# Two of the four weight-block sums of a seven-product FFN chunk pair, formed by adding transfers instead of VectorE

## The chip, the cores and the metric

The kernel runs on one core of one Trainium2 chip. The metric is the device time of one execution in microseconds (us), from repeated runs; for a one-core program that is the time of that core. Before the change the median of three runs is 2695.78 us (2693.13 to 2700.33).

## The reference

Two blocks run one after the other on a (512, 1024) activation: a first block of dilated attention and a gated linear recurrence, and two layers of FFN, token mix, FFN. The change touches only the FFN:

```
def _swiglu(h, w_gate, w_up, w_down):
    return (jax.nn.silu(h @ w_gate) * (h @ w_up)) @ w_down
...
    h = _rmsnorm(x, norm_g[l, 0]) * (1.0 + sc0) + sh0
    x = x + 0.5 * g0 * _swiglu(h, ffn_w_gate[l, 0], ffn_w_up[l, 0], ffn_w_down[l, 0])
```

There are four such FFNs (two layers, two each), with w_gate and w_up of 1024 x 2816 and w_down of 2816 x 1024, all fp32.

## The kernel before, in words

Activations lie transposed in SBUF, features on the 128 partitions and the 512 positions along the free axis. Every fp32 weight is split into a rounded part "hi" (written by ScalarE, L399) and a remainder "lo" (VectorE subtracts, L400), and a product is the sum of three passes hi*x_hi, lo*x_hi, hi*x_lo on TensorE.

Three of the four FFNs run in `ffn7` (L1343). Its 22 column blocks of 128 go two at a time; such a pair of blocks is called a chunk here. The first two chunks (blocks 0 to 3) are plain. Each of the nine others is computed by `seven` (L1391): the eight block products of [gate; up] with the two halves of the features and the two halves of the positions are replaced by seven products of 24 matmuls of 256 columns each (`prod`, L1378, matmul at L1385). With A11, A12 the two halves of the gate weights (512 features each), and p21, p22 those of the up weights, the weight-side sums are made in SBUF, on VectorE: s1 = p21 + p22 (two instructions, L1410), S3 = p21 + A11 in place (L1411), S2 = A11 + s1 in place (two, L1413), S4 = A12 + S2 in place (L1417).

Each of the seven products is a step with three stages: a load, a split (with sums ahead of it where there are any), and a run on TensorE. `ahead = 3` (L1550) puts the load stage 6 steps and the split stage 3 steps before the run stage. Between the second and the third step of the first chunk of each group of four blocks stand four `down` steps (L1483), the w_down products of the group before (matmul at L1504). So one group of two chunks is, on TensorE: A11, A12, four downs, S2, S1, S3, S4, A22, then A11', A12', S2', S1', S3', S4', A22' (a prime marks the second chunk). The groups of an `ffn7` are blocks 4-8, 8-12, 12-16, the single chunk 16-18, and 18-22: nine chunks, of which four are second in their group; in three `ffn7`, 27 chunks and 12 second ones.

Buffers: `raw` (the gate weights of a chunk, 1 MB) has 2; pieces `pc` of 512 KB (the up halves and the down weights, `piece`, L1336) rotate over 3 (`mraw` two, `macc` one); `hi` and `lo` have 4 each; `s` tiles (128x512) 40. All loads are issued by SP, in one queue, in order; a load waits there until its buffer is free, and everything behind it waits too. The order on each engine is set by the framework that places instructions, from the program's order and its own estimate of when each can start; it isn't always the order in which the code calls them. POOL has no work in the stretches of `seven`.

Of the kernel before, what the change touches and what calls it, by code (L numbers as in the profile page):

```python
# [11 lines left out]
ALU = mybir.AluOpType  # L12
# [282 lines left out]
class Prog:  # L295
# [1047 lines left out]
    def ffn7(self, l, s, h, nxt):  # L1343


        nc, A = self.nc, self.A
        wg, wu, wd = (A[f"ffn_w_{n}_2"][l, s // 2] for n in ("gate", "up", "down"))
# [30 lines left out]
        def prod(ps, w, x, first, last=True):  # L1378
            hi, lo = w
            for f in range(2):  # L1380
                cs = slice(f * 128, f * 128 + 128)
                o = ps[:, f * 256:(f + 1) * 256]
                for i, (a, b) in enumerate(((hi, x[0]), (lo, x[0]), (hi, x[1]))):
                    for k in range(4):
                        mm(o, a[:, k, cs], b[k], start=(first and f == i == k == 0), stop=(last and i == 2 and k == 3),  # L1385
                           skip_group_check=True)

        def parts():
            return [self.wp.tile([128, 4, 256], F32R, name=self.nm(n), tag=n) for n in ("hi", "lo")]

        def seven(f, dst):  # L1391

            cs = slice(f * 128, f * 128 + 256)
            u = {}

            def load_g():
                u["g"] = self.wload([(0, wg[:, cs])], KD, 256)

            def load_u():
                u["u"] = [self.piece(wu[a:a + 512, cs], 4) for a in (0, 512)]  # L1400

            def a1(i):
                return u["g"][:, 4 * i:4 * i + 4, :]

            def sums():

                p21, p22 = u["u"]
                u["s1"] = [self.s(shape=(128, 2, 256)) for _ in range(2)]
                for i in range(2):
                    nc.vector.tensor_add(u["s1"][i], p21[:, 2 * i:2 * i + 2, :], p22[:, 2 * i:2 * i + 2, :])  # L1410
                nc.vector.tensor_add(p21, p21, a1(0))  # L1411
                for i in range(2):
                    nc.vector.tensor_add(a1(0)[:, 2 * i:2 * i + 2, :], a1(0)[:, 2 * i:2 * i + 2, :], u["s1"][i])  # L1413

            def sum4():

                nc.vector.tensor_add(a1(1), a1(1), a1(0))  # L1417

            def whole(key, src, before=None):
                def g():  # L1420
                    if before:
                        before()
                    u[key] = parts()
                    self.split(src(), *u[key])
                return g

            def split1():
                u["S1"] = hi, lo = parts()
                for i in range(2):
                    self.split(u["s1"][i], hi[:, 2 * i:2 * i + 2, :], lo[:, 2 * i:2 * i + 2, :])  # L1430

            def copy(key, bank):
                u[key] = self.s()
                nc.scalar.activation(u[key], u[bank], AF.Copy)

            def run1():
                u["a"] = self.acc()
                prod(u["a"], u["A11"], forms.b11, True)
                copy("p1", "a")

            def run2():
                u["b"] = self.att()
                prod(u["b"], u["A12"], forms.b21, True)
                nc.vector.tensor_add(u["p1"], u["p1"], u["b"])

            def run6():
                prod(u["a"], u["S2"], forms.t2, False)
                copy("p2", "a")

            def run5():  # L1450
                u["c"] = self.att()
                prod(u["c"], u["S1"], forms.t1, True)
                copy("p5", "c")

            def run7():
                prod(u["a"], u["S3"], forms.t3, False)
                copy("p3", "a")
                nc.vector.tensor_add(u["p3"], u["p3"], u["p5"])

            def run3():  # L1460
                prod(u["c"], u["S4"], forms.b22, False)
                nc.vector.tensor_add(u["p2"], u["p2"], u["c"])

            def run4():
                prod(u["a"], u["A22"], forms.t4, False)

                aa = dst()
                for hf, (g, up) in ((1, (u["p2"], u["p3"])), (0, (u["p1"], u["a"]))):
                    t = self.s()
                    nc.scalar.activation(t, g, AF.Tanh, scale=0.5)  # L1470
                    nc.vector.scalar_tensor_tensor(t, t, 1.0, g, op0=ALU.add, op1=ALU.mult)
                    nc.vector.tensor_mul(t, t, up)
                    hi, lo = (d[:, hf].rearrange("p f n -> p (f n)") for d in aa)
                    nc.scalar.activation(hi, t, AF.Copy, scale=-1.0)
                    nc.vector.scalar_tensor_tensor(lo, t, -1.0, hi.bitcast(F32), op0=ALU.mult, op1=ALU.subtract)

            no = lambda: None
            return [(load_g, whole("A11", lambda: a1(0)), run1), (no, whole("A12", lambda: a1(1)), run2),
                    (load_u, whole("S2", lambda: a1(0), sums), run6), (no, split1, run5),
                    (no, whole("S3", lambda: u["u"][0]), run7), (no, whole("S4", lambda: a1(1), sum4), run3),  # L1480
                    (no, whole("A22", lambda: u["u"][1]), run4)]
# [35 lines left out]
        cs = slice(256, 512)  # L1517
# [3 lines left out]
        for m in range(2):  # L1521
            ms = slice(m * 128, m * 128 + 128)
            ps = []
            for r in range(2):
# [6 lines left out]
                p = self.acc() if r == 0 else self.att()  # L1531
# [4 lines left out]
        i = 3 * l + s + 1  # L1536
        steps, before = [], down(0, 4, aa)
        for f0, f1 in ((4, 8), (8, 12), (12, 16), (16, 18), (18, 22)):
            aa = []

            def dst(aa=aa):
                aa.append(a_tiles())
                return aa[-1]
# [624 lines left out]
```

## Time and profile before

| | |
|---|---|
| median of 3 runs | 2695.78 us |
| the profiled execution's own time | 2695.07 us |
| its span, first to last instruction | 2693.3 us |
| PE (TensorE) busy | 2605.3 us, 97% |
| DVE (VectorE) busy | 1973.2 us, 73% |
| ACT (ScalarE) busy | 1165.9 us, 43% |
| POOL busy | 322.5 us, 12% |
| moved by DMA | 339.70 MB, mean 126 GB/s |

The span is what the profile covers; 1.8 us of the execution's time lie around it. Busy shares are averages over stages that differ, so what a change is worth is read in its own stage.

### The profile page before, as it was taken

Reading aid. Unit: us, or ns where it says so; the run is one execution under the profiler, and the core shown is the slowest. Engines: PE = TensorE matmul, PEld = TensorE weight load, DVE = VectorE, ACT = ScalarE, POOL = GpSimd, SP = SyncE. Lnnn points to the kernel's source line nnn. Section 1 sums busy time; section 2 is a strip of 40 time slices with the busy share of each in tenths; the row PEclk is TensorE's granted clock in tenths of the full one; section 3 lists DMA queues with packets and bytes.
Section 4 is the critical chain, followed back from the end, with each engine's and each line's share of the span. In section 5 each row is a group of like instructions: output and inputs, shape, how many; then the busy total and the mean of one; then the engine's idle time right before and its main releaser. Section 6 shows DMA issues by size and latency. Waiting matters only on the chain.

```text
span 2693.3 us, 40840 instructions
## 1 busy us (share of the span) xinstructions
PE 2605.3 (97%) x15952; PEld 2275.8 (85%) x15952; DVE 1973.2 (73%) x3401; ACT 1165.9 (43%) x2112; POOL 322.5 (12%) x425
## 2 busy tenths in 40 slices
PE   7999989999999999999999999999999999999998
PEld 5878767789877889987889999999999887889998
DVE  8776784745878645689677778777777689677776
ACT  5322242634322224456544445444444557444434
POOL 4010010102100002232300000100002423200001
PEclk9999999999999999999999999999999999999999
DMA  9766645233467423631223324133233622123321
GB/s 274 255 203 204 229 138 187 79 114 106 152 223 242 155 88 103 178 90 50 87 66 101 116 86 148 53 106 95 90 112 89 177 63 64 56 94 102 111 94 63
DMA packets 317233, 339.70 MB, mean 126 GB/s; under 512 B 22128, under 2 KB 287856, under 8 KB 317040
## 3 DMA queue, kind: packets, MB, share of 16 engines
q1 hardware_dynamic: 317040, 337.10, 39.8%
q8 instruction: 125, 2.05, 0.3%
q14 instruction: 68, 0.56, 0.1%
HBM read 328.67 MB, written 8.39 MB: 125 GB/s over the span
## 4 chain that ended last, share of the span: by engine, by line
PE 70%; DVE 13%; DMA 10%; issue 4%; ACT 2%; POOL 1%; SPq 0%; DVEq 0%; POOLq 0%; ACTq 0%
PE att L1504 10%; PE acc L1385 9%; DMA mraw<-in_w_ada 8%; PE att L1385 7%; PE acc L417 6%; PE acc L415 6%; PE acc L419 6%; DVE lo L400 3%; DVE macc L656 2%; PE acc L467 2%; PE acc L573 2%; PE acc L575 2%; PE acc L577 2%; PE att L1955 2%; PE att L1939 1%
## 5 line engine op out<-in xcount | busy, mean ns | idle before, releaser
L399 ACT ACTIVATE hi<-raw 128x1024 fp32r<-128x1024 f32 (+2 forms) x329 | 327.0, 995 | 472.7 <-PE acc L419 137.6
L400 DVE TENSOR_TENSOR lo<-raw,hi 128x1024 fp32r<-128x1024 f32 (+2 forms) x329 | 378.9, 1154 | 114.9 <-ACT hi L399 108.6
L415 PE MATMUL acc<-s,hi 128*128 128x512 f32 x1008 | 272.6, 405 | 15.8 <-ACT s L399 7.4
L417 PE MATMUL acc<-s,lo 128*128 128x512 f32 x1008 | 266.4, 400 | 0.0
L419 PE MATMUL acc<-s,hi 128*128 128x512 f32 x1008 | 260.0, 394 | 0.0
L130 POOL TENSOR_TENSOR q<-q,q 128x256 f32<-128x256 f32 x96 | 80.6, 840 | 1482.4 <-ACT q L125 1481.3
L1385 PE MATMUL acc<-s,hi 128*128 128x256 f32 x1728 | 253.1, 281 | 0.0
L656 DVE SCALAR_TENSOR_TENSOR macc<-mraw,cs,macc 128x1024 f32<-128x1024 f32 x133 | 171.2, 1287 | 102.4 <-DMA mraw<-in_w_ada 98.7
L415 PEld LDWEIGHTS acc<-s,hi 128*128 128x128 f32 x1008 | 188.8, 191 | 61.5 <-ACT s L399 8.6
L417 PEld LDWEIGHTS acc<-s,lo 128*128 128x128 f32 x1008 | 192.0, 191 | 45.7 <-issue 0.5
L1385 PEld LDWEIGHTS acc<-s,hi 128*128 128x128 f32 x1728 | 226.4, 189 | 1.5
L419 PEld LDWEIGHTS acc<-s,hi 128*128 128x128 f32 x1008 | 189.9, 189 | 43.6
L400 DVE TENSOR_TENSOR lo<-pc,hi 128x1024 fp32r<-128x1024 f32 (+1 forms) x138 | 156.1, 1132 | 51.7 <-ACT hi L399 51.2
L1385 PE MATMUL att<-s,hi 128*128 128x256 f32 x1296 | 192.5, 281 | 0.0
L399 ACT ACTIVATE hi<-pc 128x1024 fp32r<-128x1024 f32 (+1 forms) x138 | 135.1, 981 | 109.7 <-PE att L1504 53.0
L1385 PEld LDWEIGHTS att<-s,hi 128*128 128x128 f32 x1296 | 169.9, 189 | 0.0
L1504 PE MATMUL att<-sm,hi 128*128 128x512 f32 x528 | 146.4, 393 | 0.0
L1259 DVE SCALAR_TENSOR_TENSOR x<-att,der,x 128x512 f32<-128x512 f32 x120 | 88.5, 748 | 67.6 <-PE att L1504 67.5
L1385 PE MATMUL acc<-s,lo 128*128 128x256 f32 x864 | 137.1, 280 | 0.0
L1259 DVE SCALAR_TENSOR_TENSOR x<-acc,der,x 128x256 f32<-128x256 f32 (+1 forms) x136 | 75.8, 560 | 77.3 <-PE acc L577 52.1
L1385 PEld LDWEIGHTS acc<-s,lo 128*128 128x128 f32 x864 | 117.3, 188 | 0.0
L1504 PEld LDWEIGHTS att<-sm,hi 128*128 128x128 f32 x528 | 98.5, 188 | 22.2
(491 smaller groups left out, 5485.1 us busy)
## 6 DMA issues: line engine op xcount, KB each, us to landing
mraw<-in_w_ada SPq DMA_DIRECT2D x144, 512.0 KB, 4.3
raw<-in_ffn_w_gate SPq DMA_DIRECT2D x44, 1024.0 KB, 5.2
raw<-in_w_in SPq DMA_DIRECT2D x30, 1024.0 KB, 5.5
pc<-in_ffn_w_up SPq DMA_DIRECT2D x60, 512.0 KB, 3.6
pc<-in_ffn_w_down SPq DMA_DIRECT2D x60, 512.0 KB, 3.6
raw<-in_w_in SPq DMA_DIRECT2D x46, 512.0 KB, 5.2
raw<-in_ffn_w_up SPq DMA_DIRECT2D x14, 1024.0 KB, 6.9
raw<-in_ffn_w_down SPq DMA_DIRECT2D x12, 768.0 KB, 5.2
```

What stands on the lines that cost most here:

```text
L130: nc.gpsimd.tensor_tensor(parts[-1], parts[-1], sq, op=ALU.add)
L399: self.nc.scalar.activation(hi, src, AF.Copy)
L400: self.nc.vector.tensor_sub(lo, src, hi.bitcast(F32))
L415: mm(ps, hi[:, k, :], xh[k], start=(k == 0), stop=False)
L417: mm(ps, lo[:, k, :], xh[k], start=False, stop=False)
L419: self.last_mm = mm(ps, hi[:, k, :], xl[k], start=False, stop=(k == kc - 1)).ins
L467: self.last_mm = mm(ps, x[k][:, ts], ws[k // 4][part][:, k % 4, :], start=(i == 0 and k == 0), stop=(i == 2 and k == KD - 1)).ins
L573: mm(ps, hi[k], ah[k], start=(k == 0), stop=False)
L656: nc.vector.scalar_tensor_tensor(st["acc"], raw, cs[:, k:k + 1], st["acc"], op0=ALU.mult, op1=ALU.add)
L1259: self.nc.vector.scalar_tensor_tensor(x, ps, gate[:, c:c + 1], x, op0=ALU.mult, op1=ALU.add)
L1385: mm(o, a[:, k, cs], b[k], start=(first and f == i == k == 0), stop=(last and i == 2 and k == 3), skip_group_check=True)
L1504: mm(ps.rearrange("p (a n) -> p a n", a=2), w[:, k, cs], aa[k // 2][x][:, :, k % 2, :], start=(i == k == 0), stop=(i == 2 and k == kc - 1))
```

## The change

`load_u` now brings the up weights so that two of the sums are formed by the transfers. The tile that becomes S3 is filled with p21 by SP as before, and then a transfer issued by POOL adds the A11 half of the gate weights to it, from DRAM. The two halves of s1 become `s` tiles that SP fills with p21 (a second reading of it, two loads of 256 KB), to which two POOL transfers add p22. p22 itself is still loaded by SP. The VectorE instructions of L1410 and L1411 are gone; those of L1413 and L1417 stay (in the new file they stand 8 lines further down, at L1421 and L1425, as all that follows them does).

```
             def load_u():
-                u["u"] = [self.piece(wu[a:a + 512, cs], 4) for a in (0, 512)]
+
+                up = [wu[a:a + 512, cs] for a in (0, 512)]
+                s3 = self.piece(up[0], 4)
+                u["s1"] = [self.s(shape=(128, 2, 256)) for _ in range(2)]
+                for add, ap, s3_ap in ((False, up[0], None), (True, up[1], wg[0:512, cs])):
+                    for i in range(2):
+                        src = ap[i * 256:i * 256 + 256].rearrange("(k p) n -> p k n", p=128)
+                        if add:
+                            nc.gpsimd.dma_start(u["s1"][i], src, accum_op=ALU.add)
+                        else:
+                            nc.sync.dma_start(u["s1"][i], src)
+                    if add:
+                        nc.gpsimd.dma_start(s3, s3_ap.rearrange("(k p) n -> p k n", p=128), accum_op=ALU.add)
+                u["u"] = [s3, self.piece(up[1], 4)]
...
             def sums():

-                p21, p22 = u["u"]
-                u["s1"] = [self.s(shape=(128, 2, 256)) for _ in range(2)]
-                for i in range(2):
-                    nc.vector.tensor_add(u["s1"][i], p21[:, 2 * i:2 * i + 2, :], p22[:, 2 * i:2 * i + 2, :])
-                nc.vector.tensor_add(p21, p21, a1(0))
                 for i in range(2):
                     nc.vector.tensor_add(a1(0)[:, 2 * i:2 * i + 2, :], a1(0)[:, 2 * i:2 * i + 2, :], u["s1"][i])
```

The order on the engines, in the group of blocks 8 to 12 of the first `ffn7`. First DVE, around the sums of the second chunk, before; raw_13223 holds its gate weights, pc_13288 and pc_13290 its p21 and p22, s_13383 and s_13384 the halves of s1, lo_13355 is the split of A12', lo_13391 that of S2':

```order
L1410 TENSOR_TENSOR s_13383<-pc_13288,pc_13290 128x512
L1458 TENSOR_TENSOR s_13351<-s_13351,s_13321 128x512
L1410 TENSOR_TENSOR s_13384<-pc_13288,pc_13290 128x512
L400 TENSOR_TENSOR lo_13355<-raw_13223,hi_13354 128x1024
L1462 TENSOR_TENSOR s_13286<-s_13286,att_13296 128x512
L1411 TENSOR_TENSOR pc_13288<-pc_13288,raw_13223 128x1024
L1471 SCALAR_TENSOR_TENSOR s_13420<-s_13420,s_13286 128x512
L1413 TENSOR_TENSOR raw_13223<-raw_13223,s_13383 128x512
L1413 TENSOR_TENSOR raw_13223<-raw_13223,s_13384 128x512
L1472 TENSOR_TENSOR s_13420<-s_13420,s_13351 128x512
L1471 SCALAR_TENSOR_TENSOR s_13426<-s_13426,s_13086 128x512
L400 TENSOR_TENSOR lo_13391<-raw_13223,hi_13390 128x1024
```

The three rows of L1410 and L1411 are those that go. DVE at the same place after the change; raw_13229 holds the gate weights, s_13296 and s_13297 are the halves of s1, lo_13368 is A12', lo_13399 S2', lo_13441 S1':

```order
L1466 TENSOR_TENSOR s_13364<-s_13364,s_13334 128x512
L400 TENSOR_TENSOR lo_13368<-raw_13229,hi_13367 128x1024
L1421 TENSOR_TENSOR raw_13229<-raw_13229,s_13296 128x512
L1470 TENSOR_TENSOR s_13292<-s_13292,att_13309 128x512
L1421 TENSOR_TENSOR raw_13229<-raw_13229,s_13297 128x512
L1425 TENSOR_TENSOR raw_13229<-raw_13229 128x1024
L1479 SCALAR_TENSOR_TENSOR s_13428<-s_13428,s_13292 128x512
L400 TENSOR_TENSOR lo_13399<-raw_13229,hi_13398 128x1024
L1480 TENSOR_TENSOR s_13428<-s_13428,s_13364 128x512
L1479 SCALAR_TENSOR_TENSOR s_13434<-s_13434,s_13097 128x512
L400 TENSOR_TENSOR lo_13441<-s_13296,hi_13440 128x512
```

The sum S2' (now L1421) follows A12' directly, with L1470 between its halves, and the sum S4' (now L1425) has moved up to stand right behind it.

SP's queue there, before; raw_13465 is the gate load of the next group, pc_13528 its first down piece:

```order
L1340 DMA pc_13288<-in_ffn_w_up 128x4x256
L1340 DMA pc_13290<-in_ffn_w_up 128x4x256
L387 DMA raw_13465<-in_ffn_w_gate 128x8x256
L1340 DMA pc_13528<-in_ffn_w_down 128x4x256
L1340 DMA pc_13561<-in_ffn_w_down 128x4x256
```

After the change; pc_13294 is the tile that becomes S3', pc_13303 is p22', raw_13473 the gate load of the next group:

```order
L1340 DMA pc_13294<-in_ffn_w_up 128x4x256
L1340 DMA pc_13303<-in_ffn_w_up 128x4x256
L387 DMA raw_13473<-in_ffn_w_gate 128x8x256
L1410 DMA s_13296<-in_ffn_w_up 128x2x256
L1410 DMA s_13297<-in_ffn_w_up 128x2x256
L1340 DMA pc_13536<-in_ffn_w_down 128x4x256
```

The two fills of s1 of the second chunk stand behind the gate load of the next group, though the code calls them before p22. POOL's queue in the group, where there was no row before; s_13059 and s_13060 are s1 of the first chunk, pc_13057 its S3:

```order
L1408 DMA s_13059<-in_ffn_w_up 128x2x256
L1408 DMA s_13060<-in_ffn_w_up 128x2x256
L1412 DMA pc_13057<-in_ffn_w_gate 128x4x256
L1412 DMA pc_13294<-in_ffn_w_gate 128x4x256
L1408 DMA s_13296<-in_ffn_w_up 128x2x256
L1408 DMA s_13297<-in_ffn_w_up 128x2x256
```

The adding transfers of the second chunk's s1 are the last two of the six.

## Rows read from the trace of the kernel before

**Rows 1.** Busy time per engine in the three stretches of seven-product steps.

```profile
core 0: us, PE busy (x) PEld busy (x) DVE busy (x) ACT busy (x) POOL busy (x), PEclk, DMA share, GB/s
1387.20:1665.80 278.60, 278.60 (x1942) 259.73 (x1942) 217.23 (x264) 122.27 (x163) 0.00 (x0) 1.00 0.32 102
1742.60:2021.40 278.80, 278.80 (x1944) 259.81 (x1944) 217.16 (x264) 122.27 (x163) 0.00 (x0) 1.00 0.32 102
2376.80:2654.40 277.60, 277.60 (x1944) 258.59 (x1943) 217.01 (x264) 122.43 (x163) 0.00 (x0) 1.00 0.30 96
```

**Rows 2.** Waits of PE on the work that ends a stretch (us, times, longest).

```profile
PE acc L573 <- DVE s L1472: 3.8, 3, 2.0
PE acc L573 <- ACT sm L1474: 2.9, 3, 1.5
```

**Rows 3.** Groups by line and form: DVE sums (busy us, mean ns, idle before).

```profile
L1410 DVE TENSOR_TENSOR s<-pc,pc 128x512 f32<-128x512 f32 x54 | 36.0, 686 | 4.1 <-DMA pc<-in_ffn_w_up 3.6
...
L1411 DVE TENSOR_TENSOR pc<-pc,raw 128x1024 f32<-128x1024 f32 x27 | 33.0, 1221 | 0.5
```

**Rows 4.** GB/s in 40 slices of us 1450 to 1512 (one group).

```profile
GB/s 311 1 216 145 307 123 235 0 0 0 0 0 0 0 0 0 192 146 11 26 318 351 311 9 0 0 0 0 11 0 0 0 237 102 15 268 376 330 38 11
```

**Rows 5.** Timeline of SP: start us, us issuing.

```profile
1375.36 0.37 SPq L1340 DMA_DIRECT2D pc<-in_ffn_w_down  x1
...
1442.13 0.37 SPq L1340 DMA_DIRECT2D pc<-in_ffn_w_down  x1
...
1452.28 0.37 SPq L1340 DMA_DIRECT2D pc<-in_ffn_w_up  x1
...
1479.57 0.37 SPq L387 DMA_DIRECT2D raw<-in_ffn_w_gate  x1
```

**Rows 6.** Timeline of POOL after the first stretch.

```profile
1673.31 0.74 POOL L130 TENSOR_TENSOR q<-q,q 128x256 f32<-128x256 f32 x1 [317.24 <-ACT q L125]
```

**Rows 7.** DMA issues, whole span: KB each, median us from issue to landing.

```profile
raw<-in_ffn_w_gate SPq DMA_DIRECT2D x44, 1024.0 KB, 5.2
pc<-in_ffn_w_up SPq DMA_DIRECT2D x60, 512.0 KB, 3.6
...
pc<-in_ffn_w_down SPq DMA_DIRECT2D x12, 256.0 KB, 2.6
...
s<-in_cm SPq DMA_DIRECT2D x3, 256.0 KB, 8.9
```

**Rows 8.** Timeline of DVE in the group of blocks 8 to 12.

```profile
1453.68 1.23 DVE L400 TENSOR_TENSOR lo<-pc,hi 128x1024 fp32r<-128x1024 f32 x1 [0.22 <-ACT hi L399]
...
1472.74 1.23 DVE L400 TENSOR_TENSOR lo<-pc,hi 128x1024 fp32r<-128x1024 f32 x1 [0.40 <-ACT hi L399]
...
1489.27 1.22 DVE L1411 TENSOR_TENSOR pc<-pc,raw 128x1024 f32<-128x1024 f32 x1
1490.41 0.69 DVE L1471 SCALAR_TENSOR_TENSOR s<-s,s 128x512 f32<-128x512 f32 x1
1491.01 1.29 DVE L1413 TENSOR_TENSOR raw<-raw,s 128x512 f32<-128x512 f32 x2
```

**Rows 9.** Chain of waits in the group: start us, us, what.

```profile
1454.91 22.23 PE att L1504 x96
...
1497.03 2.85 PE acc L1385 x24
```

**Rows 10.** Timeline of PE: first lo matmuls of S2' and of S1'.

```profile
1497.34 0.64 PE L1385 MATMUL acc<-s,lo 128*128 128x256 f32 x4
...
1500.19 0.63 PE L1385 MATMUL att<-s,lo 128*128 128x256 f32 x4
```

**Rows 11.** Timeline of DVE, head of the first stretch.

```profile
1387.23 0.69 DVE L1369 TENSOR_TENSOR s<-s,att 128x512 f32<-128x512 f32 x1
...
1389.52 0.68 DVE L400 TENSOR_TENSOR pT<-s,sm 128x512 fp32r<-128x512 f32 x1
```

**Rows 12.** Chain of waits, head of the first stretch: start us, us, what.

```profile
1392.88 22.21 PE att L1504 x96
```

## The prediction

> **What bounds the kernel now.** I read first the busy time by stage, since the change lives in three stretches only, the seven-product steps of the three `ffn7`. There the reader sees PE busy for 278.60 of 278.60, 278.80 of 278.80 and 277.60 of 277.60 us, with POOL at 0.00 and DVE at about 217 [rows 1]. PE's list of waits names no line of a seven-product step; the nearest are the waits of L573, the tail that follows a stretch [rows 2]. So these stretches are as long as their matmuls, and VectorE work taken out of them is taken from under a cover that stays. Then I read one group closely, blocks 8 to 12: on DVE where the sums lie, on SP when the loads leave, on PE when each product starts.
>
> **What the change removes.** 54 additions of 128x512 and 27 of 128x1024 on DVE: 36.0 + 33.0 = 69.0 us busy [rows 3], 2.6 us a chunk. On the path that sets the end this is worth 0, because PE is never idle where they run [rows 1]. The only gain in reach is at the tails, where PE waited 3.8 us for L1472 and 2.9 us for L1474 [rows 2], 6.7 us in all. I take 0 of it: the removed sums of a stretch's last chunk ran some 20 us (seven products of 2.85 us [rows 9]) before that wait, which is the latency of the last activation. Bounds: 0 to 6.7 us gained.
>
> **What it adds.** Per chunk two SP loads of 256 KB and three adding transfers on POOL, two of 256 KB and one of 512 KB: 1.5 MB more, beside the 3 MB (gate, up, half a set of down pieces) of now. The rings carry zero for long parts of a group and 376 GB/s at best [rows 4], so there is room. SP's two issues cost 0.37 us each [rows 5], in a queue that waits for buffers anyway: 0. POOL's issues delay nothing there, since its next work comes after 317.24 us of idling [rows 6]: 0. The reload of the buffers still hangs on the same splits: 0. What counts is when the sums land.
>
> **S3.** p21 of a first chunk is issued at 1452.28 [rows 5], lands 3.6 us later [rows 7], and its split on DVE runs at 1472.74 [rows 8], 17 us after landing. An added 512 KB transfer fits even at twice 3.6 us, behind the two others. Cost 0.
>
> **s1 of a second chunk: the tight place.** Both fills stand in SP's queue behind the next group's gate load, issued at 1479.57 [rows 5]. That megabyte takes 5.2 us to land [rows 7], so 1484.8. From 512 to 1024 KB costs 1.6 us (3.6 to 5.2), so 256 KB more on a busy queue costs 0.8: fills down at 1485.6 and 1486.4. Then POOL issues the two additions, in order, and DVE can do S2'.
> The deadline comes from PE. S2' starts at 1497.03, its lo matmuls at 1497.34, those of S1' at 1500.19 [rows 9, 10]. In DVE's new order S1' lo is ready when, after the second half of L1413, these have run: L1417 and the split of S2' at 1.14 us each (start to start, 1489.27 to 1490.41) and seven pieces of 0.60 us (1490.41 to 1491.01) [rows 8]: 6.5 us. So L1413 must end by 1493.7; for S2' alone, 1.14 + 0.60 + 1.14 = 2.9 us before 1497.34, 1494.5 would do. The first decides: the second addition must have landed by 1493.1, the first by 1491.9 (L1413, L1462, L1413, 0.6 us each). From 1485.6 that leaves 6.3 us for one addition and 7.5 us for both. Before, L1413 ran at 1491.01; without L1410 and L1411 DVE is there at 1488.4.
> How long does an adding transfer take? The trace has none. Below: a plain one of 256 KB, 2.6 us [rows 7]; the additions land at 1488.2 and 1489.0, lateness 0. Above: the slowest 256 KB of this kernel, 8.9 us in the crowded start [rows 7], one strictly after the other: 1485.6 + 17.8 = 1503.4, 10.3 us late. An adding transfer reads its target as well, so I take twice the plain time, 5.2 us, with the second issued while the first flies: 1490.8 and about 1491.6, both in time. It is nearest to the plain row because size, shape and engines are the same. Twice the plain time strictly in series would be 1496.0, 2.9 us late.
> The Trainium skill (Collectives: The Full Stack, "The bandwidth ceiling") says that the add in the DMA datapath costs nothing itself, but needs two source reads and so halves the rate. By it the moving part of 0.8 us would become 1.6, an addition some 3.4 us as an estimate, and two in series would still be in time; no run here shows it yet.
> There are 12 second chunks, and each anchors anew on PE's end of the downs (the gate buffer is freed by a split that waits for that), so 1 us late costs 12 us. I take 0.
>
> **s1 of a first chunk.** Fills behind the down piece issued at 1442.13 [rows 5] and what is still ahead of it land near 1449 (an estimate: 3.6 us for that piece, 0.8 for each fill, 1.6 for what is ahead); the new order puts L1413 at about 1453.5, ahead of a split that ran at 1453.68 [rows 8] for the third down, which PE reaches at 1454.91 + 2 x 5.56 = 1466 [rows 9]. Spare: over 10 us. Only the first chunk of each stretch is closer: fills issued after 1375.36 [rows 5] land near 1382, DVE comes to L1413 at 1387.2, ahead of the work for the tile split at 1389.52 [rows 11], which the downs read from 1392.88 [rows 12]. That leaves about 7 us for the additions, three times in all. Cost 0.
>
> **Another rule weighed.** An addition of 512 columns takes 686 ns on DVE and one of 1024 columns 1221 [rows 3]: 1.04 ns for each further column, and POOL shows no spans beside them that could say who blocks whom. The Trainium skill (SBUF — State Buffer, "Summary: rules for kernel authors") speaks against this change: POOL's descriptors starve while DVE is in a doubled mode, so such transfers should leave from another queue. Yet the same page's "Who interferes with whom" gives additions of two tensors no such mode, and by that the rate in the row is the single one. I give it a small chance as rival B.
>
> **Sum.** 2695.07 - 0 + 0: the profiled execution is 0.7 us under the median of 2695.78, so I name 2696.
>
> **The rivals.**
> A. *The second chunk's additions land late* (slower). Place: L1413 of the second chunk, DVE waiting with L1462, L1471 and the splits of S2' and S1' behind it, then PE. It decides when the two additions take over 7.5 us from the fills' landing. Price 12 us for each us late: series at twice the plain time 2.9 x 12 = 35 us, 2731; the upper bound 10.3 x 12 = 124 us, 2820. For it: both go through one queue that had no work, and the fills stand behind a megabyte. Against: 2.6 us for the plain 256 KB.
> B. *POOL is held up by DVE* (slower): each issue waits for the instruction in hand, up to 1.22 us, two issues 2.4 us. With in-series additions of 5.2 us the lateness becomes 5.3 us: 64 us, 2760. With mine, 1491.6 + 2.4 = 1494.0, 0.9 us late: 11 us, 2707.
> C. *The relief of DVE reaches the tails and heads* (faster): at most the 6.7 us there, 2689, and over 0.3% only if the heads give something too.
> D. *The extra traffic delays plain loads* (slower): a gate or down piece late by 1 us in each of 15 groups, 15 us, 2711. Against it the empty slices [rows 4].
> That the change doesn't do what it says is excluded: 81 DVE rows are gone from the order, 81 POOL rows and 54 SP rows are new.
>
> **How the numbers follow.** 0.3% is 8 us, about what a measurement of this kernel tells from no change. Forecast (all hidden, or under 0.7 us late per second chunk) 0.60; A 0.30; B 0.04; D 0.03; C 0.03. So faster 0.03, same 0.60, slower 0.37. The forecast's own range is 2691 to 2704. The whole range takes in A up to the series case and a little beyond, 2735; above it some 0.14 of A, B and D is left out, below 2691 0.03.
>
> **What would show it.** Right: PE full in the three stretches, DVE about 69 us less busy, 81 POOL transfers of 3 to 6 us to landing, DVE's waits for them at L1421 short and with no PE wait behind. Wrong: PE waiting at L1385 for lo or hi of S2' or S1', 12 times with a like length (A), or 27 times (then first chunks are late too, and an addition takes over 10 us); POOL's issues stretched while DVE works (B).

## The result and the profile after

| | before | after |
|---|---|---|
| median, runs beside each other (4 and 4) | 2698.06 us | 2726.84 us |
| ratio, 95% interval | | 1.0116 [1.0098, 1.0133] |
| the profiled execution's own time | 2695.07 us | 2726.2 us |
| its span | 2693.3 us | 2724.4 us |
| DVE busy | 1973.2 us | 1906.9 us |
| POOL busy | 322.5 us | 421.8 us |
| moved by DMA | 339.70 MB | 382.20 MB |

The kernel is 1.2% slower. The time lies in the whole range of the prediction, which took in rival A; the likeliest case, 2696, was not the one that came. DVE did lose what was foretold (66.3 us against 69.0), and the three stretches got longer all the same.

First the stretches, by windows that run (to about 0.1 us) from the first matmul of the seven-product line to the first one of the tail (columns as in [rows 1]):

```profile
1384.00:1678.20 294.20, 283.92 (x1945) 263.87 (x1944) 195.87 (x237) 123.68 (x164) 31.02 (x25) 0.98 0.59 145
1754.40:2044.60 290.20, 281.23 (x1945) 261.43 (x1944) 196.08 (x237) 124.15 (x164) 31.05 (x25) 0.99 0.58 144
2396.50:2685.10 288.60, 280.33 (x1944) 260.51 (x1943) 195.43 (x238) 123.55 (x163) 31.03 (x25) 0.99 0.57 140
```

Before, PE was busy for every microsecond of them [rows 1]. Now it lacks 10.3, 9.0 and 8.3 us, and is itself busy 5.3, 2.4 and 2.7 us longer for the same matmuls. Taken exactly from the one matmul's start to the other's, the three together grow from 836.0 to 873.7 us. The waits of PE name the cause of the gaps:

```profile
PE acc L1385 <- ACT s L1442: 26.7, 12, 5.3
...
PE acc L573 <- DVE s L1480: 5.2, 3, 1.7
```

Twelve waits, one for each second chunk (columns as in [rows 2]). They are on an ACT copy, L1442, which the prediction never mentions. The tail waits are about those of before.

The new work itself, by groups of lines and then by issues to landing (last column: median us):

```profile
L1408 POOL DMA_DIRECT2D s<-in_ffn_w_up x54 | 65.8, 1404 | 599.4 <-DMA s<-in_ffn_w_up 517.5 <-PE att L417 27.6 <-DVE s L1368 27.5
L1421 DVE TENSOR_TENSOR raw<-raw,s 128x512 f32<-128x512 f32 x54 | 37.3, 690 | 75.6 <-DMA s<-in_ffn_w_up 75.6
L1412 POOL DMA_DIRECT2D pc<-in_ffn_w_gate x27 | 34.9, 1292 | 186.5 <-DMA pc<-in_ffn_w_up 92.0 <-DVE lo L400 58.1 <-DVE x L1259 23.0
```

```profile
raw<-in_ffn_w_gate SPq DMA_DIRECT2D x44, 1024.0 KB, 5.4
pc<-in_ffn_w_up SPq DMA_DIRECT2D x60, 512.0 KB, 3.9
pc<-in_ffn_w_down SPq DMA_DIRECT2D x60, 512.0 KB, 4.9
...
s<-in_ffn_w_up SPq DMA_DIRECT2D x54, 256.0 KB, 5.9
s<-in_ffn_w_up POOLq DMA_DIRECT2D x54, 256.0 KB, 5.7
pc<-in_ffn_w_gate POOLq DMA_DIRECT2D x27, 512.0 KB, 6.7
```

An adding transfer of 256 KB lands 5.7 us after its issue (the median of 54, from 4.3 to 8.3), one of 512 KB 6.7 us; DVE stands 75.6 us in front of L1421. The chain of waits in the group of blocks 8 to 12, the one that the prediction followed, shows how this gets to PE (start, us, what):

```profile
1477.85 0.37 SPq L387
...
1478.31 5.81 DMA s<-in_ffn_w_up
...
1484.68 0.49 POOL s L1408
...
1485.39 5.95 DMA s<-in_ffn_w_up
...
1491.37 0.70 DVE raw L1421
...
1492.10 1.23 DVE raw L1425
1493.32 0.60 DVE s L1479
1493.92 1.13 DVE lo L400
1495.06 0.61 DVE s L1480
...
1495.69 0.03 ACT pT L1482
...
1496.23 0.59 ACT s L1442
...
1496.86 3.11 PE acc L1385 x24
```

The timeline of PE has the beginning and the end of A12', the product before S2':

```profile
1492.32 0.64 PE L1385 MATMUL att<-s,hi 128*128 128x256 f32 x4
...
1494.68 0.63 PE L1385 MATMUL att<-s,hi 128*128 128x256 f32 x4
```

Read the chain from the bottom. S2' starts at 1496.86; A12' had ended at 1495.31, so PE stood 1.54 us. S2' adds into the accumulator bank of A11', and before it may do so ACT must have copied p1' out of that bank (L1442). The bank had been ready since A11' ended at 1492.47, but in ACT's queue the copy stands behind L1482, the rounding of the first chunk's activation, and L1482 waits for DVE's L1480, and L1480 stands in DVE's queue behind L1421, which waits for the second addition. So a late addition holds up work of another chunk on DVE, through that the head of ACT's queue, and through that PE. From the start of the second L1421 to S2' it is 1496.86 - 1491.37 = 5.49 us, and it is 5.5 us in eleven of the twelve places (the twelfth, with another order on DVE, is told further down).

The waits differ in length. Three of the twelve, each with the idle time at its end:

```profile
1433.00 0.74 PE L1385 MATMUL acc<-s,hi 128*128 128x256 f32 x4 [1.21 <-ACT s L1442]
1496.86 0.74 PE L1385 MATMUL acc<-s,hi 128*128 128x256 f32 x4 [1.54 <-ACT s L1442]
1661.69 1.23 PE L1385 MATMUL acc<-s,hi 128*128 128x256 f32 x4 [4.82 <-ACT s L1442]
```

The last group of each stretch (blocks 18 to 22) waits 4.82, 5.32 and 3.27 us, the nine others 1.0 to 2.4. The last row's 1.23 us for four matmuls, instead of 0.74, shows a second cost. By windows, the wait, the product S2' behind it and the product after that (the column behind POOL's is the granted clock):

```profile
1656.87:1661.69 4.82, 0.01 (x1) 0.00 (x0) 4.79 (x8) 3.26 (x6) 0.00 (x0) 0.84 0.00 0
1661.69:1667.20 5.51, 5.51 (x26) 5.51 (x27) 5.28 (x8) 2.48 (x3) 0.00 (x0) 0.52 0.25 78
1667.20:1670.00 2.80, 2.80 (x26) 2.80 (x25) 1.22 (x1) 1.54 (x2) 0.00 (x0) 1.00 0.71 210
```

The granted clock is 0.52 in the stretch behind this wait, nearly all of it at the lower level of 1.2 GHz, and S2' takes 5.29 us (to the next product at 1666.98), where 2.85 is its price [rows 9]. That happened behind four of the twelve waits (1.91, 4.82, 5.32, 3.27 us; the other three products took 4.43 to 4.47 us from start to start), so 7.2 us in all. The gaps are 27.5 us: the 26.7 in front of S2', and 0.8 in front of a down product in the last group of the first stretch (L1512 at 1633.94). That makes 34.7 of the 37.7 us. Of the last 3.0, 1.9 are overlap lost: rows of four matmuls last 0.64 us and follow each other every 0.47 us, and behind a wait nothing overlaps, so that by starts the twelve S2' came 28.6 us late and not 26.7. The rest, about 1 us, is spread thinly. The rest of the program reads 6.6 us shorter in this profile than in that of before, and 1846 to 1860 us over all profiles of this study; what sets that is left open.

### The profile page after: what moved, and what is told of

It is laid out like the page before. It is cut to its first block, busy times and chain, and to the rows that moved or that the text cites. A ratio compares the mean times of both kernels' runs of the same rounds, so it can differ in the third digit from the quotient of the medians.

```text
span 2724.4 us, 41068 instructions
## 1 busy us (share of the span) xinstructions
PE 2612.3 (96%) x15952; PEld 2279.3 (84%) x15952; DVE 1906.9 (70%) x3320; ACT 1169.0 (43%) x2112; POOL 421.8 (15%) x506
## 2 busy tenths in 40 slices
DMA packets 360867, 382.20 MB, mean 140 GB/s; under 512 B 24288, under 2 KB 331488, under 8 KB 360672
## 4 chain that ended last, share of the span: by engine, by line
PE 64%; DMA 14%; DVE 13%; issue 4%; ACT 2%; POOL 2%; SPq 1%; DVEq 0%; POOLq 0%; ACTq 0%
PE att L1512 10%; DMA mraw<-in_w_ada 7%; DMA s<-in_ffn_w_up 6%; PE acc L1385 6%; PE acc L417 6%; PE acc L419 6%; PE acc L415 6%; PE att L1385 4%; DVE lo L400 3%; DVE macc L656 2%; PE acc L467 2%; PE acc L573 2%; PE acc L575 2%; PE acc L577 2%; PE att L1963 1%
## 5 line engine op out<-in xcount | busy, mean ns | idle before, releaser
L400 DVE TENSOR_TENSOR lo<-raw,hi 128x1024 fp32r<-128x1024 f32 (+2 forms) x329 | 378.8, 1154 | 107.4 <-ACT hi L399 106.3
L1385 PE MATMUL acc<-s,hi 128*128 128x256 f32 x1728 | 259.3, 285 | 26.7 <-ACT s L1442 26.7
L400 DVE TENSOR_TENSOR lo<-pc,hi 128x1024 fp32r<-128x1024 f32 (+1 forms) x138 | 155.9, 1131 | 49.0 <-ACT hi L399 48.9
L1408 POOL DMA_DIRECT2D s<-in_ffn_w_up x54 | 65.8, 1404 | 599.4 <-DMA s<-in_ffn_w_up 517.5
L1512 PE MATMUL att<-sm,hi 128*128 128x512 f32 x528 | 146.4, 393 | 0.0
```

The lines of the kernel that those rows point to most:

```text
L400: self.nc.vector.tensor_sub(lo, src, hi.bitcast(F32))
L1408: nc.gpsimd.dma_start(u["s1"][i], src, accum_op=ALU.add)
L1512: mm(ps.rearrange("p (a n) -> p a n", a=2), w[:, k, cs], aa[k // 2][x][:, :, k % 2, :], start=(i == k == 0), stop=(i == 2 and k == kc - 1))
```

## The experiments

Theory A, formed on this trace: additions of second chunks land too late for DVE's queue, and the delay goes through ACT's queue to PE. Its rivals are the extra traffic itself, POOL held up by DVE, and the transfer for S3. In the table, "stretches" is the sum of the three, from the first matmul of the product line to the first of the tail.

| run | ratio to before, 95% | stretches, us | waits on the copy of p1' |
|---|---|---|---|
| before | | 836.0 | none |
| the change | 1.0116 [1.0098, 1.0133] | 873.7 | 12, 26.7 us |
| e1 fills early | 1.0081 [1.0059, 1.0104] | 866.4 | 7, 21.8 us |
| e6 copy first | 1.0027 [1.0013, 1.0042] | 839.4 | 4, 2.3 us |
| e4 dummy traffic | 1.0042 [1.0027, 1.0057] | 843.0 | none |
| e2 S3 only | 0.9995 [0.9981, 1.0009] | 836.0 | none |
| e11 fills first, all | 1.0128 [1.0108, 1.0148] | 871.3 | 11, 14.9 us |
| e5 S4 late | 1.0066 [1.0046, 1.0086] | 853.3 | 5, 6.9 us |
| e3 s1 only | 1.0114 [1.0087, 1.0141] | 867.0 | 12, 23.5 us |
| e9 control | 1.0004 [0.9991, 1.0016] | 836.0 | none |
| e13 early, held | 1.0025 [1.0011, 1.0039] | 846.1 | 3, 4.6 us |
| e14 all mended | 1.0012 [1.0000, 1.0024] | 839.3 | 2, 2.8 us |

**e6: ACT's queue.** The changed kernel; the first chunk's rounding is queued behind the next chunk's copy. Fills and additions keep their places in the queues. (The lo part that belongs to the rounding, L1483 on DVE, moves back with it; it stands behind everything on the way to the copy in both kernels.)

```
 def run1():
...
-    copy("p1", "a")
+    p1 = copy("p1", "a")
+    while late:
+        with self.tc.issue_after(p1.ins):
+            late.pop(0)()        # L1482, L1483 of the chunk before
```

> The changed kernel with ACT's queue altered at one place per second chunk: the copy of p1' out of its accumulator bank stands ahead of the first chunk's rounding of its activation (L1482), instead of behind it. Fills and additions land as late as in the changed kernel. If the link from the late additions to PE is ACT's in-order queue (the copy waiting behind L1482, which waits for DVE), PE's wait for S2' falls from 1.5 us to about 0.5 us or nothing in the middle groups, and the time to 2698 to 2710. If the additions are simply too late for S2' itself whatever ACT does, the waits only change their name, to DVE or ACT of the split of S2', and the time stays at 2720 to 2730.

Measured 2701.2 us, against 2694.2 for before beside it. The rows of ACT at the same place (the copy is L1443 here, the rounding L1488), and PE's waits:

```profile
1486.69 1.14 ACT L399 ACTIVATE hi<-s 128x512 fp32r<-128x512 f32 x2
1487.74 0.58 ACT L1443 ACTIVATE s<-acc 128x512 f32<-128x512 f32 x1
1489.24 0.63 ACT L1488 ACTIVATE pT<-s 128x512 fp32r<-128x512 f32 x1 [0.93 <-DVE s L1484]
```

```profile
PE acc L573 <- DVE s L1484: 12.0, 3, 5.3
...
PE acc L1386 <- ACT s L1443: 2.3, 4, 0.8
```

The second sum of S2' began at 1484.92 and S2' was due at 1489.40, 4.48 us later; with 5.49 us between them, as in the change, PE would have stood 1.0 us. It did not stand. Swapping two ACT instructions gives back 34 of the 37.7 us of the stretches, with every transfer where it was in its queue. The link through ACT is shown, and so is that the additions were not too late for the operands of S2' themselves. What is left of the 7 us against before is 3.4 us of the stretches and longer waits at the tails: all of PE's waits at L573 are 13.5 us here, 9.8 before.

**e9: the same edit without the change.** The kernel before with e6's edit.

> Control: the kernel before, with the same edit of ACT's queue as in the run with the copy first (the copy of p1' ahead of the first chunk's rounding of its activation), no transfer changed. PE has no wait there to lose, so the time of before, 2692 to 2700 us. If it were faster by some microseconds, the gain of the run with the copy first would not all be a mended wait.

Measured 2696.7 us, 1.0004. The edit has no gain of its own, so what e6 gave back was the wait and what hung on it.

**e2 and e3: the two halves of the change.** In e2 only S3 is formed by a transfer, and s1 is added by DVE into the tiles that SP fills. In e3 only s1 is formed by transfers.

```
 e2, in sums():
...
     for i in range(2):
+        nc.vector.tensor_add(u["s1"][i], u["s1"][i], u["u"][1][:, 2 * i:2 * i + 2, :])
 e3, in sums():
...
+    nc.vector.tensor_add(u["u"][0], u["u"][0], a1(0))
```

> Half of the change: S3 is formed by the adding transfer, s1 by DVE as before (in place on a tile that SP fills with p21, since p21's own tile is being added to). The late fills stay, but DVE adds as soon as they have landed, one transfer earlier than in the change. Theory A: the fills alone land by about 1485.5 in the group of blocks 8 to 12, before DVE comes to the sums, so 2695 to 2703 us. Rival (S3's addition, 6.7 us and the largest of the three, is what costs): about 2720 or more, with waits on S3's split.

> Half of the change: s1 by transfers, S3 on DVE as before. The framework then puts DVE's work around S2' in the same order as in the run with S4 late (S4 behind the split of S2), so that is the run to compare with. Theory A (only s1 is late, S3's transfer is free): the same time as that run within 4 us, 2705 to 2714, with waits in the last groups. If S3's 512 KB on POOL's queue and the rings add to the lateness: 2695 to 2703.

e2 measured 2691.8 us, 0.9995, and PE is full in the first stretch as it was before:

```profile
1390.00:1668.60 278.60, 278.60 (x1943) 259.73 (x1941) 206.90 (x255) 123.83 (x164) 11.71 (x9) 1.00 0.49 136
```

e3 measured 2726.6 us, outside what was expected, because its premise was wrong: the framework left S4 ahead of the split of S2', as in the changed kernel, and with the changed kernel it is to be compared: 12 waits of 23.5 us against 12 of 26.7, 1.0114 against 1.0116. By the ratios the whole loss comes with s1 (by the stretches of the two profiles, 31.0 of the 37.7 us); S3's transfer, the largest of the three, costs nothing by itself (e2), and neither do fills that land late.

**e5: DVE's queue.** The sum S4 (L1425), which the change had let move up, is queued behind the split of S2 again.

```
...
-    nc.vector.tensor_add(a1(1), a1(1), a1(0))
+    with self.tc.issue_after(u["S2lo"]):
+        nc.vector.tensor_add(a1(1), a1(1), a1(0))
```

> The changed kernel with the sum S4 (L1425) queued on DVE behind the split of S2, about where it stood before the change. All transfers unchanged, fills and additions as late as in the change. Theory A through ACT's queue: between the end of the second L1421 and the rounding L1482 there now stand three 0.6 us pieces instead of 1.14 + 0.60 + 1.14 + 0.60, so each of the 12 waits shrinks by up to 1.7 us: the seven or eight of 1.0 to 1.5 us go, the last groups keep 1.5 to 3.6 us, and the time is 2705 to 2714 us. If DVE's order had nothing to do with it: 2727.

Measured 2712.9 us. In the group of blocks 8 to 12 the second L1421 starts at 1492.59 and the copy ends at 1496.76, 4.2 us instead of 5.5, and PE waits only 0.1 us there. Of the nine waits outside the last groups one of 1.26 us is left beside some of under 0.2 us, and of the 37.7 us of the stretches 17.3. In two of the last groups PE now waited for A12' as well (3.6 us).

**e4: the traffic alone.** The kernel before, and beside it the same bytes into tiles that nobody reads.

```
 in load_u():
...
+    for i in range(2):
+        nc.sync.dma_start(d[i], src[0][i])
+    for i in range(2):
+        nc.gpsimd.dma_start(d[i], src[1][i], accum_op=ALU.add)
+    for i in range(2):
+        nc.gpsimd.dma_start(d[i], src[2][i], accum_op=ALU.add)
...
```

> The kernel before, with all its VectorE sums, and beside them the change's whole extra traffic into tiles that nobody reads: per chunk two SP fills of 256 KB, two adding transfers of p22 and two of the gate half (256 KB each). Theory A: nothing waits for them, so the time of before, 2695 to 2703 us, with no PE wait at the seven-product line. Rival D (the traffic itself, on the rings, on SP's queue or in SBUF): 2710 to 2730. Rival B would show as DVE additions of more than 690 and 1220 ns or as POOL issues stretched far over 1.2 us.

Measured 2705.6 us, between the two theories. The row of DVE's waits that is new in size:

```profile
DVE s L1421 <- DMA pc<-in_ffn_w_up: 34.2, 15, 3.7
```

In this kernel L1421 is the old sum of p21 and p22; its waits for these pieces were 3.6 us in all before [rows 3]. The up pieces land in 5.2 us instead of 3.6, and in the last groups that gets through to PE. So rival D is real, though small: 7 us of the stretches. It bears less on the change itself, whose s1 does not wait for the p22 tile: e14 below carries all of the traffic at 1.0012. DVE was busy for 1973.3 us against 1973.2 before, so these transfers did not stretch its instructions.

**e1 and e11: fills ahead of the megabyte.** e1 queues a chunk's gate load behind the fills issued before it; e11, whose lines stand here, does so with every 1 MB weight load.

```
+    self.fill = nc.sync.dma_start(u["s1"][i], src).ins
...
 in wload():
+    with self.tc.issue_after(self.fill) if getattr(self, "fill", None) else contextlib.nullcontext():
```

> The changed kernel with one edge more: each gate load is queued on SP behind the s1 fills of the chunk before it, so that the two fills of a second chunk leave before the next group's megabyte (about 1473 instead of 1478.3 in the group of blocks 8 to 12) and the additions land about 5 us or more earlier. Everything moved stays the same: same bytes, same 81 adding transfers, same removed VectorE sums. Theory A (the second chunk's additions land late, and DVE, ACT and PE queue behind them): the 12 waits of PE on the copy of p1' go away and the time is that of before, 2695 to 2705 us. Rival D (the extra bytes and transfers themselves slow the kernel): still about 2727. Rival B (POOL's issues held up by DVE): POOL's issues still take 1.2 us or more, and the time goes down only because they start earlier.

> The run with fills ahead of the gate load left its longest waits (8.9, 4.9, 3.8 us) in the last group of each stretch, where the megabyte ahead of the fills is the first weight load of the next stage's head and not a gate load of a chunk. Here every 1 MB weight load is queued behind the s1 fills issued before it in the program. Theory A (the fills' place behind a megabyte): these three waits go or fall below 2 us, and with them the slower products behind them, so 2697 to 2705 us. If the last group's waits have another cause (its half-length downs leave too little time for any adding transfer), they stay above 3 us and the time at 2712 to 2720.

Both missed: 2717.9 and 2730.3 us. In e1 the last groups keep 17.6 of its 21.8 us of waits. In two of them the fills still leave behind a megabyte, the first weight load of the next stage, which the edit does not reach: the second sum begins 3.6 us after S2' is due in the first stretch and 0.5 us before it in the second. Outside the last groups the additions landed early, and the waits fell from 13.3 to 4.3 us; in the group of blocks 8 to 12 PE hardly waited. But DVE's rows there show another order:

```profile
1481.55 0.69 DVE L1426 TENSOR_TENSOR raw<-raw,s 128x512 f32<-128x512 f32 x1 [1.75 <-DMA s<-in_ffn_w_up]
1482.16 0.69 DVE L1471 TENSOR_TENSOR s<-s,s 128x512 f32<-128x512 f32 x1
1482.77 1.22 DVE L400 TENSOR_TENSOR lo<-raw,hi 128x1024 fp32r<-128x1024 f32 x1
```

The framework, which now placed the sums sooner, has them ahead of the split of A12' (the L400 row). All that stood between the second sum and L1482 before still does, and four more instructions, the two rows shown behind the sum among them: from this sum's start to the end of the copy it is 1490.41 - 1481.55 = 8.9 us. In the change it is 5.5. So the additions came earlier, and were needed earlier too. In e11 every group has this order, and in its last groups PE even waited for A12' itself (7.7 us, 3 times).

**e13: the fills early and DVE's order held.** e11, with the sums queued behind the split of A12'. DVE's order around S2' is then the changed kernel's; SP's order differs.

```
+    with self.tc.issue_after(u["A12lo"]):
         nc.vector.tensor_add(a1(0)[:, 2 * i:2 * i + 2, :], ...)
```

> The two runs with the fills moved ahead changed two things: the fills' place on SP, and DVE's order, where the framework then put the sums L1421 ahead of the split of A12', so that everything behind them waited longer. Here the fills are ahead of every megabyte as before, and the sums are held behind the split of A12', so that DVE's order around S2' is that of the changed kernel again; only SP's order differs from it. Theory A (second chunk's additions late): landing about 4 us earlier in the middle groups, whose waits (1.0 to 2.4 us) go; about 2 us earlier in the last groups, whose waits shrink from 3.3 to 5.3 us to 1 to 3 us; 2700 to 2712 us. If DVE's order was not what spoiled the two earlier runs: 2717 to 2730 as there.

Measured 2701.3 us. POOL and DVE in the same group:

```profile
1472.75 2.42 POOL L1410 DMA_DIRECT2D s<-in_ffn_w_up  x2 [14.14 <-DMA s<-in_ffn_w_up]
```

```profile
1482.23 0.69 DVE L1424 TENSOR_TENSOR raw<-raw,s 128x512 f32<-128x512 f32 x1
1482.84 0.68 DVE L1474 TENSOR_TENSOR s<-s,att 128x512 f32<-128x512 f32 x1
1483.43 0.68 DVE L1424 TENSOR_TENSOR raw<-raw,s 128x512 f32<-128x512 f32 x1
```

DVE no longer waits for the additions there, all nine waits outside the last groups are gone, and the last groups keep 2.25, 1.96 and 0.40 us. In those nine places DVE's order is as in the change, and an earlier landing takes the waits away: the time of landing is shown to be a cause, by a second road. Beside e11 it shows too that the order was what had spoiled the early fills.

**e14: all mended.** e13 with e5's and e6's edits.

> All repairs together on the changed kernel: fills ahead of the megabytes, sums held behind the split of A12', S4's sum behind the split of S2, and the copy of p1' ahead of the first chunk's rounding on ACT. Theory A: no wait of more than 1 us at the seven-product line, the three stretches together within 5 us of those of before (836.0 us), and 2692 to 2701 us: the change cost nothing but the wait, and gains nothing either, since PE is full there. If the freed VectorE time were worth something on the path that sets the end, it would show here as a time under 2690 us.

Measured 2698.6 us, 1.0012 [1.0000, 1.0024]. Two waits of 1.3 and 1.5 us remain, both in a last group; none of over 1 us was expected:

```profile
PE acc L1388 <- ACT s L1448: 2.8, 2, 1.5
```

The 68 us that DVE has less to do than before (1904.9 against 1973.2 us busy) buy nothing, since PE is full. No version beat the kernel before by more than a measurement can tell.

## Why the prediction was wrong in its likeliest case, step by step

**What bounds the kernel: right.** PE was full, and work taken from DVE there was worth 0. e2 and e14 show it with 31 and 68 us of DVE work gone.

**S3: right.** It cost 0 (e2).

**s1 of a second chunk, the landing: 1.6 us short.** From the fills' landing to that of the second addition I had 6.0 us (1485.6 to 1491.6); it took 7.2 (1484.12 to 1491.34). An addition was put at 5.2 us. Here the first took 4.7 us and the second, which decides, 6.0; and I gave no time to the some 0.5 us from the fills' landing to the first issue. The other 0.4 us are the fills, which landed 11.0 us before S2' was due and not 11.4. S2' was due at 1495.16: A12' began at 1492.32, and a product takes 2.84 us there. So the landing was foretold 5.4 us ahead of S2' (1497.03 - 1491.6) and came 3.8 us ahead (1495.16 - 1491.34).

**s1 of a second chunk, the deadline: the step that failed.** "The first decides: the second addition must have landed by 1493.1", that is 3.9 us ahead of S2'. I followed only DVE's rows to the lo parts of S2' and S1'. By that deadline what came would have been about enough: 3.8 us here, and 2.9 to 4.3 over the nine second chunks outside the last groups, 3.9 in the median. In e6 the second sums there begin 3.4 to 4.7 us ahead, and PE waits once in nine, for 0.2 us. The true need was 5.5 us, for two things left out: S2' goes on in the bank of A11', so the copy of p1' on ACT must come first; and that copy stands behind L1482, which hangs on DVE's L1480. The order that I had shown myself has L1425 ahead of these, 1.14 us of the 5.5 (e5 gave back 1.3). Rival A's own threshold failed for the same cause: it asked for over 7.5 us from the fills, and 7.2 was late.

**s1 of a first chunk: right but for the last groups.** "Spare: over 10 us", cost 0. In the last group of a stretch the downs are half as long, and the chain of the changed kernel ahead of the 4.82 us wait runs through a first chunk's addition:

```profile
1623.05 7.02 DMA s<-in_ffn_w_up
...
1630.10 0.04 DVE raw L1421
...
1641.79 1.22 DVE lo L400
...
1643.03 0.37 SPq L387
...
1643.49 5.62 DMA s<-in_ffn_w_up
```

DVE runs late from 1630.10 on (PE waits 0.8 us for it at 1633.94), the split that frees the gate buffer ends at 1643.01, and only then do the gate load and the fills leave, 13.7 us before S2' is due (1656.70) where the group of blocks 8 to 12 had 17.3. In the second stretch's last group it is 14.5 us, without a first chunk's addition in the chain. So in these two the second sum begins 0.5 and 0.02 us before S2' is due. The third stretch's last group is another case: its second sum begins 5.6 us ahead, which would just have done, but there the framework had put the sums ahead of the split of A12' (the L400 row), the order of the e1 rows above, and from that sum to S2' it is 8.9 us:

```profile
2660.57 0.69 DVE L1421 TENSOR_TENSOR raw<-raw,s 128x512 f32<-128x512 f32 x1 [1.08 <-DMA s<-in_ffn_w_up]
2661.18 0.69 DVE L1466 TENSOR_TENSOR s<-s,s 128x512 f32<-128x512 f32 x1
2661.78 1.22 DVE L400 TENSOR_TENSOR lo<-raw,hi 128x1024 fp32r<-128x1024 f32 x1
```

These three groups alone make 13.4 of the 26.7 us. They are a term of their own, and I had none.

**Rival A: right in place, sign and count.** Twelve waits, one in each second chunk, in eleven of them with the fills behind a megabyte. "12 us for each us late" gave 2731 by a lateness of 2.9 us in each; it was 26.7 us in 12 unequal waits (2.2 us in the mean), with 7.2 us on top for the clock, which the price had not, and with 6.6 us less in the rest of the program. That 2731 lies so near to 2726.8 is luck: the condition of that price, two additions of 5.2 us one after the other, did not hold, and the link to PE was not the one that A named. The forecast's 0.60 against A's 0.30 was too bold: predicted landing and true deadline lay 0.1 us apart (5.4 against 5.5).

**Rival B: no.** POOL's issues of 256 KB took 1179 to 1725 ns, whatever DVE did: with DVE busy for over nine tenths of an issue that stood by itself it took 1188 to 1237 ns, with DVE idle 1188; those of 1518 and more were the second of a pair and overlapped the first. DVE's sums kept their 690 ns beside 686 before. The rule of the Trainium skill (SBUF — State Buffer, "Summary: rules for kernel authors") that POOL's descriptors starve beside DVE in a doubled mode shows no effect with these additions. **Rival C: no** (e14). **Rival D: small** (7 us of the stretches in e4); the prediction had put the room on the rings at no cost.

The Trainium skill's rule on the add in the transfer (Collectives: The Full Stack, "The bandwidth ceiling"), by which two reads halve the rate, would have made an addition some 3.4 us, by the estimate that I worked out from it. Measured are 5.7 us for 256 KB and 6.7 for 512 in the median, 4.3 and 5.8 for the fastest: the further 256 KB cost 1.0 to 1.5 us, so most of the time is not in the bytes, and halving the rate says little of an addition of this size.

## What to carry to other kernels

The deadline of an operand is not found on its own engine alone: ask what else the consumer needs (here a bank that another engine must empty), in whose in-order queue that stands, and whether the late instruction is ahead of it there. Work taken off an engine that isn't the bound pays nothing, and a DMA put in its place adds a latency (here some 6 to 7 us) that each queue behind it inherits. And an earlier arrival must be read together with the new order: a scheduler that expects data sooner may move the waiting instruction forward and undo the gain.

## What the runs showed that I had not expected

- A POOL issue of an adding transfer took about the same for 256 KB (median 1.2 us) and 512 KB (1.3 us), so two halves, 2.42 us one behind the other, cost nearly twice the issue of a whole; SP's issues took 0.37 us [rows 5].
- A wait of PE cost more than its length where the granted clock fell: 0.50 to 0.62 over the next product, which then took 4.4 to 5.3 us instead of 2.85. It fell behind waits of 1.91, 3.27, 4.82 and 5.32 us, and not behind one of 2.40 us (at 2446.64, whose product ran at 1.00 in 2.93 us). In other runs it fell behind 2.25 us (e13) and not behind 2.03 and 2.69 us (e3), so the length of the wait alone does not decide; what does was not tried.
- Additions landed later where a plain megabyte flew beside them. For the twelve second chunks the first addition took 4.6 us and the second 5.9 in the change (medians); in e13, where a gate load was in flight in ten of the twelve, 6.7 and 8.5.
